# A hybrid block on one core: the second row tile scaled in two parts, a weight half rounded on another engine, rows turned together, and two Silus put off

## The chip, the cores and the metric

The program runs on one core of a Trainium2 chip. The metric is the device time of one execution in microseconds (us), the median of several runs. The core has five engines that each run their own queue in order: TensorE (PE; its weight loads are shown as PEld), VectorE (DVE), ScalarE (ACT), GpSimd (POOL) and SyncE (SP), which here only issues DMA transfers.

## What is computed

The reference is a decoder block on a residual stream x of 512 rows by 1024 columns. Cut to its stages:

```python
h = rmsnorm(x, norm1_g[l])
z = h @ w_in[l] + b_in[l]
z_glu, z_rx, z_rg, z_ga, z_gb = jnp.split(z, split_idx, axis=-1)
u = silu(layernorm(causal_depthwise_conv(glu(z_glu))))
y_a = u @ conv_w_out[l] + conv_b_out[l]
xb = causal_depthwise_conv(z_rx, lru_conv_w[l], lru_conv_b[l])
hb = rg_lru(xb, lru_wa[l], lru_ba[l], lru_wx[l], lru_bx[l], lru_lambda[l])
y_b = (hb * gelu(z_rg)) @ lru_w_out[l]
x = x + (sigmoid(z_ga) * y_a + sigmoid(z_gb) * y_b) @ w_mix_out[l]
h = rmsnorm(x, norm2_g[l])
x = x + (silu(h @ ffn_w1[l]) * (h @ ffn_w3[l])) @ ffn_w2[l]
return rmsnorm(x, norm_f_g)
```

Everything is float32. rg_lru has 16 heads of 80 columns, each with its own 80 by 80 gate weights and biases lru_ba and lru_bx; the channel mixer is 2816 wide.

## The kernel before

**Products.** Each float32 factor is split in a rounded high part and a low part (`split_to`, `first_parts`): a cast makes the high part, a subtraction the low part. A float32 product is then three products on TensorE: high by high, high by low, low by high (`mm3`). Names that end in h and l are these parts. Weights come in chunks of 128 by 1024 numbers: `load_chunk` loads a chunk to one of four `raw` buffers through SP's queue, `emit_chunk` makes its parts in one of five `hl` buffers, casts mostly on ScalarE, subtractions on POOL or DVE. `in0` is the first chunk of w_in; its parts are made in halves (`first_parts`, L131): first half cast on DVE (L133), subtracted on POOL (L119); then second half cast and subtracted on POOL.

**The start.** x lies in four row tiles of 128 rows (`xt`; the first three are in the `wsums` pool). Tiles 0 and 1 are normalised first: the sums of squares on DVE (`half_sum`) and ScalarE (`root`), the scaling by half tiles (`scale_half`, on DVE L672 or on ScalarE L670), then eight blocks of 128 by 128 per tile are turned by TensorE (`turn_rows`, L635) into PSUM banks. `spot` says where block c goes: with six banks, blocks 0 and 3 share bank 0, and 4 and 7 share bank 3. From there `turned_parts` makes h10h to h17h on ScalarE (L644) and h10l to h17l on DVE (L645), with the norm's weights from `par`. Thirteen products of ones (`warm`, L543) run on TensorE before that. `early_first` (L689) then takes the 24 products of the first chunk on the first 256 rows in an order that follows the arrival of their parts.

**Parameters.** The per-channel vectors are loaded as rows (`rowt`, `load_rows`) and turned by TensorE (`rows_turned`, L552) to columns of `par`: the 8 rows of norm1_g at the start, the other 400 later in four blocks, and a fifth block (L555) with lru_ba and lru_bx, which has a tile of its own (`heads_b`, named rowsh).

**Order.** Inside `tc.manual_schedule` the named engines keep the order of the code; elsewhere a scheduler orders by its own model and hands out buffer slots. `tc.issue_after(i)` queues what follows behind instruction i on its engine.

**The channel mixer** runs in steps k of 256 columns. Each step of class `Seven` takes seven products of half the size instead of eight (r1 to r7, 24 products on TensorE each), for which sums of weight quarters are made beforehand in pieces: `piece_load`, four sums (`piece_sums`), `piece_store` to DRAM. `out_step` walks these pieces for the last stage (`or`): the store of one, the sums of the next, the load of one more, the DMAs on POOL's queue. In a step, `first` combines r1 and r2 to c11, and `rest` makes q, c12 and c21; `out_of` applies the Silu on ScalarE (L1443) and multiplies on DVE (L1444). Weights for later products are cast on ScalarE meanwhile.

Of the kernel before, what the change touches and what calls it, by code (L numbers as in the profile page):

```python
# [13 lines left out]
P = 128  # L14
T = 512
# [13 lines left out]
NF = DF // P  # L29


SLOTS, SHORT = 63, 5
RAW = 4
HL = 5
AHEAD = 4
SUMS_BEHIND = 3
WARM = 13

PACK = HB // 2
ROWS_G = HB + PACK  # L40
# [4 lines left out]

PIECES = 3


OUT_PIECES = {0: "1", 1: "111", 2: "01", 3: "11", 4: "111", 5: "101", 6: "111", 7: "111", 8: "101", 9: "101", 10: "100"}
# [34 lines left out]
def tile_block(ctx, tc, a, out):  # L86
# [43 lines left out]

    def first_parts(h, l, full):  # L131
        for cs in (slice(0, T), slice(T, 2 * T)):
            (pool_e if cs.start else vec).tensor_copy(h[:, cs], full[:, cs])  # L133
            newest["sub"] = sub(pool_e, l[:, cs], full[:, cs], h[:, cs].bitcast(F32)).ins
        return h, l

# [361 lines left out]
        at += n  # L498
    rowt = [longt(f"rows{b}") for b in range(row_at(n_rows - 1)[0] + 1)]

    heads_b = longt("rowsh")

    pool_e.memset(heads_b[: 2 * NH, :P], 0.0)

    def load_head_rows():
        for g, name in enumerate(("lru_ba", "lru_bx")):
            nc.sync.dma_start(heads_b[g * NH : (g + 1) * NH, :HB], a[name][0].rearrange("(h p) -> h p", p=HB))

    def load_rows(i, queue=nc.sync):
        lo, m, src = parts[i]  # L510
# [1 line left out]
        queue.dma_start(rowt[b][r : r + m, :P], src)  # L512

    x_nat = a["x"].rearrange("b (t p) d -> p (b t) d", p=P)
    wide = [wsums.tile([P, 1024], F32, tag="wsum", name=f"x{t}") for t in range(PIECES)]
    xt = [[w[:, :T], w[:, T:]] for w in wide] + [[longt(f"x{t}{h}") for h in range(2)] for t in range(PIECES, NT)]

    def load_x(t):
        if t < PIECES:
# [19 lines left out]


    wp = bank2("warm")
    for _ in range(WARM):
        pe.matmul(wp[:, :P], ones, ones, start=True, stop=True)  # L543

    load_x(0)
    load_x(1)

    def rows_turned(c0, c1):
        pt = bank2(f"par_ps{c0}")
        for c in range(c0, c1, P):  # L550
            m = min(P, c1 - c)
            pe.transpose(pt[:, c - c0 : c - c0 + m], rowt[row_at(c)[0]][:m, :P], ident[:m, :m])  # L552
        at = T - 2 * NH
        if c0:
            pe.transpose(pt[:, at:], heads_b[: 2 * NH, :P], ident[: 2 * NH, : 2 * NH])  # L555
        (vec.tensor_copy if c0 else act.copy)(par[:, c0:c1], pt[:, : c1 - c0])
        if c0:
            act.activation(bh, pt[:HB, at:], AF.Copy, scale=0.5)

    def pc(name, i):  # L560
        return par[:, col[name] + i : col[name] + i + 1]
# [67 lines left out]
    def turn_rows(t, ps, half=None):  # L629

        some = (range(ND), (0, 3, 1, 2, 4, 7, 5, 6))[len(ps) == 6]
        for c in some if half is None else some[4 * half : 4 * half + 4]:
            b, at = spot(c, ps)
            at += P * (t % 2)
            pe.transpose(ps[b][:, at : at + P], xt[t][c // 4][:, (c % 4) * P : (c % 4 + 1) * P], ident)  # L635
# [71 lines left out]
    with tc.manual_schedule(engines={ET.PE, ET.Activation, ET.DVE, ET.SP, ET.Pool}):  # L707

        turned = [(bank if q < 5 else bank2)(f"tx0{q}") for q in range(6)]
        r0 = first_sums(0)  # L710
        vec.reciprocal(r0, r0)
        r1 = first_sums(1)
        scale_half(0, 0, r0)
        turn_rows(0, turned, 0)
        scale_half(0, 1, r0, True)
        rows_turned(0, n_first)
        vec.reciprocal(r1, r1)
        scale_half(1, 0, r1)
# [10 lines left out]
        early_first(lambda: (turn_rows(1, turned, 1), turned_parts(0, turned, range(4, ND))))  # L729
# [639 lines left out]

    def out_step(k):  # L1370
        due_sums(True)
        if out_at[1]:
            with tc.issue_after(newest["full"]):
                out_stores.append(piece_store(*out_at[1], pool_e).ins)
        if out_at[0]:
            sums_due.append([SUMS_BEHIND, out_at[0]])
        out_at[1], out_at[0] = out_at[0], None
# [39 lines left out]
    def f_product(k, got, ps, x_, w_, again=False, ahead=AHEAD, between=None):  # L1417
# [3 lines left out]
        for i in range(2):  # L1421
# [17 lines left out]
                emit_to(emitted[0] + 1)  # L1439
            due_sums()  # L1440

    def out_of(c, dst):
        act.activation(c[:, LO], c[:, LO], AF.Silu)  # L1443
        newest["now"] = vec.tensor_tensor(out=dst, in0=c[:, LO], in1=c[:, HI], op=ALU.mult).ins  # L1444

    class Seven:
# [36 lines left out]
        def rest(self):  # L1483
# [5 lines left out]
            act.copy(q, r1)  # L1489
            f_product(k, got, r5, "s1", "t1")  # L1490
            add(q, r5, q)
            c12 = shortt(f"c12_{k}")
# [58 lines left out]
    for k in range(KF):  # L1551
        if k in SEVEN:
            b = begun.pop(k, None)
            if not b:
                b = Seven(k)
                b.half()
                b.first()
                out_step(k)
            b.rest()
            continue  # L1560
# [145 lines left out]
```

## Time and profile before

| what | value |
|---|---|
| runs, us | 792.69, 788.48, 790.12; median 790.12 |
| profiled execution, us | 787.58 |
| its span, first to last instruction, us | 785.8 |
| mean granted TensorE clock | 0.999 |
| busy DVE, ACT, POOL, us | 679.3, 473.5, 362.9 |
| weight and sum DMA, mean | 253 GB/s |

The profile is of one execution. A row of the timeline or of the chain of waits gives start and duration in us, the engine, the line and the tile; in brackets behind a row of the timeline stands the idle time of the engine before it and what ended it. A matmul's duration is its latency, since products overlap: the distance from one start to the next is what it costs.

### The profile page before, as it was taken

The page shows a single profiled execution, that of the slowest core. Times are in us where ns is not written, and L with a number is a line of the kernel's source. Part 1 is how long each engine was busy: PE and PEld are TensorE (multiplying, and loading weights), DVE is VectorE, ACT ScalarE, POOL GpSimd, SP SyncE. Part 2 cuts the span into 40 slices and gives each one's busy share as a digit, 9 for nine tenths or more (in the row PEclk, how much of TensorE's full clock was granted, in tenths as well). Part 3 has the DMA queues.
Part 4 walks back from the last instruction along what each step waited for, and adds up shares of the span by engine and source line. Part 5 has one row for each costly group of instructions (what it writes and reads, how often), then busy time and mean ns, then how long its engine had stood idle before and what let it go on. Part 6 is the DMA issues. An engine that isn't in the chain of part 4 may idle for free.

```text
span 785.8 us, 12508 instructions
## 1 busy us (share of the span) xinstructions
PE 778.2 (99%) x4328; PEld 680.6 (87%) x4328; DVE 679.3 (86%) x1074; ACT 473.5 (60%) x696; POOL 362.9 (46%) x353
## 2 busy tenths in 40 slices
PE   9999999999999999999999999999999999999996
PEld 8988888888888888888888898999999999888885
DVE  6389998889987987999799869897887889999956
ACT  7543678966785786574245676445445555556844
POOL 4367876789788989754530380122323322000000
PEclk9999999999999999999999999999999999999999
DMA  7657989899999868998978575699999999878652
GB/s 225 189 144 211 267 225 269 230 277 272 260 266 280 266 195 251 309 299 285 314 252 297 172 216 181 193 306 307 308 335 331 314 315 318 268 235 278 194 172 108
DMA packets 188561, 199.04 MB, mean 253 GB/s; under 512 B 15290, under 2 KB 149586, under 8 KB 188498
## 3 DMA queue, kind: packets, MB, share of 16 engines
q1 hardware_dynamic: 178066, 161.80, 67.4%
q0 software_dynamic: 10272, 36.18, 13.9%
q8 instruction: 34, 0.56, 0.3%
q14 instruction: 29, 0.24, 0.1%
q10 hardware_dynamic: 160, 0.27, 0.1%
HBM read 146.30 MB, written 38.80 MB: 236 GB/s over the span
## 4 chain that ended last, share of the span: by engine, by line
PE 99%; DVE 0%; ACT 0%; issue 0%
PE z L573 36%; PE fr L1432 25%; PE or L1195 13%; PE yb L573 7%; PE ya L573 6%; PE mxr L1195 5%; PE f L573 3%; PE g L1021 2%; PE fr L1477 1%; PE warm L543 1%; PE tx L635 0%; PE th L618 0%; PE z L689 0%; ACT of L1647 0%; PE orl L1195 0%; PE par_ps L552 0%
## 5 line engine op out<-in xcount | busy, mean ns | idle before, releaser
L821 DVE SCALAR_TENSOR_TENSOR cv<-u,par,cv 128x507 f32<-128x507 f32 (+15 forms) x240 | 162.2, 733 | 4.2 <-ACT cv L817 3.3
L119 POOL TENSOR_TENSOR hl_in<-raw_in,hl_in 128x1024 fp32r<-128x1024 f32 (+1 forms) x52 | 123.3, 2382 | 54.5 <-ACT hl_in L123 40.7
L119 POOL TENSOR_TENSOR fws<-fws 128x256 f32<-128x256 f32 x114 | 92.4, 812 | 38.9 <-DMA fws<-in_ffn_w_dram 33.4
L413 POOL DMA_DIRECT2D ot<-fwso x21 | 15.4, 732 | 140.9 <-DVE fwso L119 140.9
L1432 PE MATMUL fr<-hs_0h,hl_ft 128*128 128x256 f32 x320 | 59.2, 283 | 0.0
L119 DVE TENSOR_TENSOR hl_ft<-raw_ft,hl_ft 128x1024 fp32r<-128x1024 f32 x39 | 47.6, 1219 | 6.1 <-ACT hl_ft L123 6.0
L123 ACT CAST hl_in<-raw_in 128x1024 fp32r<-128x1024 f32 x50 | 51.4, 1047 | 1.3 <-PE z L573 1.1
L1432 PEld LDWEIGHTS fr<-hs_0h,hl_ft 128*128 128x128 f32 x320 | 50.6, 192 | 0.0
L123 ACT CAST hl_ft<-raw_ft 128x1024 fp32r<-128x1024 f32 x40 | 41.2, 1044 | 10.8 <-PE fr L1432 7.9
L1432 PE MATMUL fr<-hs_0l,hl_ft 128*128 128x256 f32 x160 | 45.3, 283 | 0.0
L123 ACT CAST hl_fb<-raw_fb 128x1024 fp32r<-128x1024 f32 x30 | 31.4, 1048 | 20.1 <-DMA raw_fb<-in_ffn_w_dram 9.3
L573 PE MATMUL z<-h10h,hl_in 128*128 128x512 f32 (+1 forms) x108 | 41.1, 382 | 0.0
L573 PE MATMUL z<-h13h,hl_in 128*128 128x512 f32 (+1 forms) x108 | 40.8, 379 | 0.0
L573 PE MATMUL z<-h14h,hl_in 128*128 128x512 f32 (+1 forms) x108 | 40.8, 379 | 0.0
L573 PE MATMUL z<-h15h,hl_in 128*128 128x512 f32 (+1 forms) x108 | 40.8, 379 | 0.0
L573 PE MATMUL z<-h16h,hl_in 128*128 128x512 f32 (+1 forms) x108 | 40.8, 379 | 0.0
L573 PE MATMUL z<-h12h,hl_in 128*128 128x512 f32 (+1 forms) x108 | 40.8, 379 | 0.0
L573 PE MATMUL z<-h11h,hl_in 128*128 128x512 f32 (+1 forms) x108 | 40.8, 379 | 0.0
L573 PE MATMUL z<-h17h,hl_in 128*128 128x512 f32 (+1 forms) x108 | 40.8, 379 | 0.0
L119 POOL TENSOR_TENSOR hl_ot<-raw_ot,hl_ot 128x1024 fp32r<-128x1024 f32 x1 | 2.4, 2405 | 82.8 <-ACT hl_ot L123 82.8
L123 ACT CAST hl_ob<-raw_ob 128x1024 fp32r<-128x1024 f32 (+1 forms) x23 | 23.4, 1016 | 23.8 <-PE or L1195 12.6
L119 DVE TENSOR_TENSOR hl_fb<-raw_fb,hl_fb 128x1024 fp32r<-128x1024 f32 x29 | 35.3, 1221 | 2.4 <-ACT hl_fb L123 2.4
(948 smaller groups left out, 2635.7 us busy)
## 6 DMA issues: line engine op xcount, KB each, us to landing
raw_in<-in_w_in_dram SPq DMA_DIRECT2D x51, 512.0 KB
fws<-in_ffn_w_dram SPq DMA_DIRECT2D x38, 512.0 KB
raw_ft<-fs SPq DMA_DIRECT2D x34, 512.0 KB
fs<-fws POOLq DMA_DIRECT2D x25, 512.0 KB, 5.7
fwso<-in_ffn_w_dram POOLq DMA_DIRECT2D x42, 256.0 KB, 7.1
ot<-fwso POOLq DMA_DIRECT2D x21, 512.0 KB, 5.3
raw_ob<-in_ffn_w_dram SPq DMA_DIRECT2D x33, 256.0 KB
raw_ot<-ot SPq DMA_DIRECT2D x33, 256.0 KB
```

The source lines that it names most:

```text
L119: return eng.tensor_tensor(out=o, in0=x, in1=y, op=ALU.subtract)
L123: copy(h, full)
L413: return queue.dma_start(dest, raw.rearrange("p (m n) -> p m n", n=256))
L543: pe.matmul(wp[:, :P], ones, ones, start=True, stop=True)
L573: pe.matmul(ps, l, r, start=i == 0, stop=i == n - 1)
L821: vec.scalar_tensor_tensor(out=acc[:, s:], in0=u[c][:, : T - s], scalar=dw(c, s), in1=acc[:, s:], op0=ALU.mult, op1=ALU.add)
L1021: pe.matmul(ps[:HB], head_chunk[0][:ROWS_G, g, h % 2, m, :], ext[h][m][:ROWS_G], start=m == 0, stop=m == 1)
L1195: pe.matmul(banks[i][:, cs], l_[:, ts], r_[:, cs], start=start and n == 0, stop=stop and n == 2, skip_group_check=again)
L1432: pe.matmul(ps[:, HALVES[i]], lw[:, c, :], rx_, start=not (again or i or c or m), stop=bool(i and c == 3 and m == 2), skip_group_check=True,)
L1477: pe.matmul(self.r4[:, HALVES[i]], lw, rx_, start=not (i or c or m), stop=bool(i and c == 3 and m == 2), skip_group_check=True)
```

## The change

Its parts, in the order of the program:

- The warm products are cut in 8 and 5. Between them the 8 rows of norm1_g are turned, into the upper half of the sixth bank of `turned` instead of a bank of their own, and ScalarE copies them to `par` behind the first root instead of behind the scaling of tile 0.
- `turned` has seven banks; blocks 0 to 3 have one each, and 4 and 7 share one.
- The first half of tile 1 is scaled in two parts of 256 columns (`scale_part`), each followed by the turning of its two blocks; the second half of both tiles is turned behind that.
- The first half of in0's high part is cast by ScalarE instead of DVE.
- lru_ba and lru_bx are loaded to rows 32 to 63 of the last row tile, which has 16 rows of conv_dw_w, and turned with it in one block of 64 rows. Their own tile is gone.
- The pool of pieces has four buffers instead of three, the pool of long tiles 61 instead of 63.
- `out_step` issues the load of a piece ahead of the store, and loads run one piece further ahead.
- `left_over`: the Silu and multiplication of c11, and in most steps of c21, are put off until behind a later copy on ScalarE.

```diff
-SLOTS, SHORT = 63, 5
+SLOTS, SHORT = 61, 5
-WARM = 13
+WARM, WARM_LATER = 13, 5
-PIECES = 3
+PIECES = 4
     def first_parts(h, l, full):
         for cs in (slice(0, T), slice(T, 2 * T)):
-            (pool_e if cs.start else vec).tensor_copy(h[:, cs], full[:, cs])
+            (pool_e.tensor_copy if cs.start else act.copy)(h[:, cs], full[:, cs])
...
-    heads_b = longt("rowsh")
-
-    pool_e.memset(heads_b[: 2 * NH, :P], 0.0)
+    h_row = 2 * NH
+    pool_e.memset(rowt[-1][: 2 * h_row, :P], 0.0)
...
-            m = min(P, c1 - c)
+            m = 2 * h_row if c0 and c1 - c <= h_row else min(P, c1 - c)
             pe.transpose(pt[:, c - c0 : c - c0 + m], rowt[row_at(c)[0]][:m, :P], ident[:m, :m])
-        at = T - 2 * NH
-        if c0:
-            pe.transpose(pt[:, at:], heads_b[: 2 * NH, :P], ident[: 2 * NH, : 2 * NH])
+        at = c - c0 + h_row
...
-        return ((c % 4, c // 4 * 256), ((0, 1, 2, 0, 3, 4, 5, 3)[c], c in (3, 7) and 256))[len(ps) == 6]
+        return ((c % 4, c // 4 * 256), ((0, 1, 2, 3, 4, 5, 6, 4)[c], c == 7 and 256))[len(ps) == 7]
...
+    def scale_part(t, cs, r):
+        vec.tensor_scalar(out=xt[t][0][:, cs], in0=xt[t][0][:, cs], scalar1=r, scalar2=None, op0=ALU.mult)
...
         r0 = first_sums(0)
+        rows_turned(0, n_first, turned[5][:, 256:])
+        warm_products(WARM_LATER)
+        turned.append(bank2("tx06"))
         vec.reciprocal(r0, r0)
         r1 = first_sums(1)
         scale_half(0, 0, r0)
-        turn_rows(0, turned, 0)
+        turn_rows(0, turned, 0, 4)
         scale_half(0, 1, r0, True)
-        rows_turned(0, n_first)
         vec.reciprocal(r1, r1)
-        scale_half(1, 0, r1)
-        turn_rows(1, turned, 0)
+        for q in range(2):
+            scale_part(1, slice(256 * q, 256 * q + 256), r1)
+            turn_rows(1, turned, 2 * q, 2)
+        scale_half(1, 1, r1)
         emit_to(1)
-        scale_half(1, 1, r1)
-        turn_rows(0, turned, 1)
+        turn_rows(0, turned, 4, 4)
...
     def out_step(k):
         due_sums(True)
-        if out_at[1]:
-            with tc.issue_after(newest["full"]):
-                out_stores.append(piece_store(*out_at[1], pool_e).ins)
...
-            with tc.issue_after(([newest["full"]] * 2 + out_stores)[out_n[0]]):
+            with tc.issue_after(([newest["full"]] * 3 + out_stores)[out_n[0]]):
                 out_at[0] = piece_load(name, halves, pool_e), dest
             out_n[0] += 1
+        if stored:
+            with tc.issue_after(newest["full"]):
+                out_stores.append(piece_store(*stored, pool_e).ins)
...
+    left = []
+
+    def left_over(behind):
+        while left:
+            with tc.issue_after(behind):
+                out_of(*left.pop(0))
...
             self.c11 = shortt(f"c11_{self.k}")
-            act.copy(self.c11, self.r1)
+            left_over(act.copy(self.c11, self.r1).ins)
...
-    def first(self):
+    def first(self, wait=False):
             add(self.c11, self.r2, self.c11)
-            out_of(self.c11, self.uv[0][:, LO])
+            if wait:
+                left.append((self.c11, self.uv[0][:, LO]))
+            else:
+                out_of(self.c11, self.uv[0][:, LO])
...
-            act.copy(q, r1)
+            left_over(act.copy(q, r1).ins)
...
-            out_of(c21, v_[:, LO])
+            if k + 1 in SEVEN and k + 1 not in BEGUN + BEGUN_LATER:
+                left.append((c21, v_[:, LO]))
+            else:
+                out_of(c21, v_[:, LO])
```

Three places show how instructions move. The first is ScalarE's queue at the start, from the squares of tile 1 (n1j10) to the first rounded row block (h10h); the numbers behind names are buffers. Before:

```order
L661 ACTIVATE n1j10_191,stats_158<-x1_123 128x512
L662 ACTIVATE stats_158<-stats_158 128x1
L670 ACTIVATE x0_122<-x0_122,stats_158 128x512
L556 COPY par_114<-par_ps0_200 128x8
L644 ACTIVATE h10h_159<-tx00_177,par_114 128x256
```

Now:

```order
L560 COPY par_114<-tx05_176 128x8
L664 ACTIVATE n1j10_193,stats_152<-x1_122 128x512
L665 ACTIVATE stats_152<-stats_152 128x1
L676 ACTIVATE x0_121<-x0_121,stats_152 128x512
L133 CAST hl_in0_213<-raw_in0_210 128x512
L647 ACTIVATE h10h_153<-tx00_171,par_114 128x256
```

The copy of the parameters stands ahead of tile 1's squares, and the cast of the first weights' half has come between the scaling of tile 0 and h10h. Before, that cast stood in DVE's queue between the two scalings of tile 1.

The second place is SP's queue where the parameters' rows are loaded (rows1 to rows4) and the next weight chunks (raw_in16 is the fifth). Before, the end of these loads:

```order
L512 DMA rows1_116<-in_norm2_g_dram 8x128
L512 DMA rows1_116<-in_lru_conv_w_dram 16x128
L512 DMA rows2_117<-in_lru_conv_w_dram 24x128
L512 DMA rows2_117<-in_conv_dw_w_dram 104x128
L512 DMA rows3_118<-in_conv_dw_w_dram 128x128
L512 DMA rows4_119<-in_conv_dw_w_dram 16x128
L168 DMA raw_in16_526<-in_w_in_dram 128x8x128
```

Now, their beginning:

```order
L168 DMA raw_in9_229<-in_w_in_dram 128x8x128
L508 DMA rows4_119<-in_lru_ba_dram 16x80
L508 DMA rows4_119<-in_lru_bx_dram 16x80
L168 DMA raw_in16_525<-in_w_in_dram 128x8x128
L513 DMA rows1_116<-in_b_in_dram 52x128
L513 DMA rows1_116<-in_conv_dw_b_dram 8x128
```

The weight chunk raw_in16 has moved past the thirteen transfers of b_in to conv_dw_w.

The third place is ScalarE's queue in the channel mixer, where step 6 follows step 5 (fr are the products' banks, ft and fb weight chunks). Before:

```order
L1443 ACTIVATE c21_5_6040<-c21_5_6040 128x256
L1463 COPY c11_6_6118<-fr1_6_6087 128x512
L123 CAST hl_ft10_6_6122<-raw_ft10_6_6120 128x1024
L1443 ACTIVATE c11_6_6118<-c11_6_6118 128x256
L123 CAST hl_ft11_6_6172<-raw_ft11_6_6170 128x1024
L123 CAST hl_fb11_7_6190<-raw_fb11_7_6187 128x1024
L1489 COPY q_6_6221<-fr1_6_6087 128x512
```

Now:

```order
L1478 COPY c11_6_6115<-fr1_6_6084 128x512
L1458 ACTIVATE c21_5_6039<-c21_5_6039 128x256
L123 CAST hl_ft10_6_6121<-raw_ft10_6_6119 128x1024
L123 CAST hl_ft11_6_6169<-raw_ft11_6_6167 128x1024
L123 CAST hl_fb11_7_6187<-raw_fb11_7_6184 128x1024
L1507 COPY q_6_6218<-fr1_6_6084 128x512
L1458 ACTIVATE c11_6_6115<-c11_6_6115 128x256
```

The Silu of c21 (step 5) goes behind the copy of c11, and that of c11 from between two casts to behind the copy of q.

More of the change, by code (lines that the diff above doesn't have):

```diff
@@ L514, in tile_block @@
     x_nat = a["x"].rearrange("b (t p) d -> p (b t) d", p=P)
-    wide = [wsums.tile([P, 1024], F32, tag="wsum", name=f"x{t}") for t in range(PIECES)]
-    xt = [[w[:, :T], w[:, T:]] for w in wide] + [[longt(f"x{t}{h}") for h in range(2)] for t in range(PIECES, NT)]
+    WIDE = 3
+    wide = [wsums.tile([P, 1024], F32, tag="wsum", name=f"x{t}") for t in range(WIDE)]
+    xt = [[w[:, :T], w[:, T:]] for w in wide] + [[longt(f"x{t}{h}") for h in range(2)] for t in range(WIDE, NT)]
     def load_x(t):
-        if t < PIECES:
+        if t < WIDE:
             nc.sync.dma_start(wide[t], x_nat[:, t, :])
@@ L541, in tile_block, with warm_products, rows_turned @@
     wp = bank2("warm")
-    for _ in range(WARM):
-        pe.matmul(wp[:, :P], ones, ones, start=True, stop=True)
+    def warm_products(n):
+        for _ in range(n):
+            pe.matmul(wp[:, :P], ones, ones, start=True, stop=True)
+    warm_products(WARM - WARM_LATER)
     load_x(0)
     load_x(1)
-    def rows_turned(c0, c1):
-        pt = bank2(f"par_ps{c0}")
+    def rows_turned(c0, c1, pt=None):
+        if pt is None:
+            pt = bank2(f"par_ps{c0}")
         for c in range(c0, c1, P):
-            m = min(P, c1 - c)
+            m = 2 * h_row if c0 and c1 - c <= h_row else min(P, c1 - c)
             pe.transpose(pt[:, c - c0 : c - c0 + m], rowt[row_at(c)[0]][:m, :P], ident[:m, :m])
-        at = T - 2 * NH
-        if c0:
-            pe.transpose(pt[:, at:], heads_b[: 2 * NH, :P], ident[: 2 * NH, : 2 * NH])
+        at = c - c0 + h_row
         (vec.tensor_copy if c0 else act.copy)(par[:, c0:c1], pt[:, : c1 - c0])
         if c0:
-            act.activation(bh, pt[:HB, at:], AF.Copy, scale=0.5)
+            act.activation(bh, pt[:HB, at : at + h_row], AF.Copy, scale=0.5)
     def pc(name, i):
@@ L625, in spot, with turn_rows @@
     def spot(c, ps):
-        return ((c % 4, c // 4 * 256), ((0, 1, 2, 0, 3, 4, 5, 3)[c], c in (3, 7) and 256))[len(ps) == 6]
-    def turn_rows(t, ps, half=None):
-        some = (range(ND), (0, 3, 1, 2, 4, 7, 5, 6))[len(ps) == 6]
-        for c in some if half is None else some[4 * half : 4 * half + 4]:
+        return ((c % 4, c // 4 * 256), ((0, 1, 2, 3, 4, 5, 6, 4)[c], c == 7 and 256))[len(ps) == 7]
+    def turn_rows(t, ps, at=0, n=None):
+        for c in range(ND) if n is None else (0, 1, 2, 3, 4, 7, 5, 6)[at : at + n]:
             b, at = spot(c, ps)
@@ L728, in tile_block @@
         turned_parts(0, turned, range(4))
-        early_first(lambda: (turn_rows(1, turned, 1), turned_parts(0, turned, range(4, ND))))
+        early_first(lambda: (turn_rows(1, turned, 4, 4), turned_parts(0, turned, range(4, ND))))
         r2 = half_sum(2)
@@ L1371, in out_step @@
         due_sums(True)
-        if out_at[1]:
-            with tc.issue_after(newest["full"]):
-                out_stores.append(piece_store(*out_at[1], pool_e).ins)
-        if out_at[0]:
-            sums_due.append([SUMS_BEHIND, out_at[0]])
-        out_at[1], out_at[0] = out_at[0], None
+        stored, begun_ = out_at[1], out_at[0]
+        if begun_:
+            sums_due.append([SUMS_BEHIND, begun_])
+        out_at[1], out_at[0] = begun_, None
         steps = out_steps.get(k)
@@ L1556, in tile_block @@
                 b.half()
-                b.first()
+                b.first(True)
                 out_step(k)
```

3 lines of the change are left out of this document (2 added, 1 removed).

## The prediction

> **What bounds the kernel now.** I read the page's first part, then the chain of waits, then the timeline of the first 13 us, where most of the edit lies, and of one step of the channel mixer, where the rest lies.
>
> ```profile
> span 785.8 us, 12508 instructions
> PE 778.2 (99%) x4328; PEld 680.6 (87%) x4328; DVE 679.3 (86%) x1074; ACT 473.5 (60%) x696; POOL 362.9 (46%) x353
> ```
> ```profile
> 1.09 5.48 PE warm L543 x26
> 6.57 0.42 issue
> ...
> 7.62 0.15 PE par_ps L552
> ...
> 9.58 2.96 PE z L689 x23
> ...
> 15.41 1.75 PE tx L635 x16
> ...
> 22.91 0.49 PE par_ps L552 x4
> 23.40 0.08 PE par_ps L555
> ...
> 499.17 175.68 PE fr L1432 x1464
> ```
> TensorE is the bound: 778.2 of 785.8 us, and what it isn't busy is 1.09 us before the first instruction, 0.42 us at 6.57 and the tail. Busy could hide stalls, so I divide: 1464 products of 256 columns in 175.68 us are 0.120 us each over the whole channel mixer. Products this even leave nothing that other engines could give back. So an edit can win only where TensorE still waits, before 12.5 us, or by taking products away. It can lose anywhere.
>
> **The start.** The next rows decide the first chunk: who releases the first real product, and who the last ones.
>
> ```profile
> 6.78 0.71 ACT L670 ACTIVATE x<-x,stats 128x512 f32<-128x512 f32 x1
> 7.11 0.48 DVE L672 TENSOR_SCALAR x<-x,stats 128x512 f32<-128x512 f32 x1
> 7.51 0.42 DVE L133 CAST hl_in<-raw_in 128x512 fp32r<-128x512 f32 x1
> 8.01 1.45 POOL L119 TENSOR_TENSOR hl_in<-raw_in,hl_in 128x512 fp32r<-128x512 f32 x1 [6.58 <-DVE hl_in L133]
> 8.24 0.47 ACT L644 ACTIVATE h10h<-tx,par 128x256 fp32r<-128x256 f32 x1 [0.26 <-PE tx L635]
> 10.10 1.29 POOL L119 TENSOR_TENSOR hl_in<-raw_in,hl_in 128x512 fp32r<-128x512 f32 x1
> 11.20 0.61 ACT L138 CAST hl_in<-raw_in 128x512 fp32r<-128x512 f32 x1
> 11.44 0.19 PEld L689 LDWEIGHTS z<-h14h,hl_in 128*128 128x128 f32 x1
> ```
> Today the row tile x1 is scaled from 7.11 to 7.59, is turned, and ScalarE, which had stood 0.26 us for it, rounds h10h from 8.24 to 8.71; the first product follows at once. Scaled in parts of 256 columns, the first part should take between half of 0.48 us and the whole, say 0.33, so turning starts some 0.15 us sooner; with four banks for the first four blocks, h10h also waits for one block of its bank instead of two. The parameters' turning (0.15 us) has left this place. The two together, and ScalarE free of the parameters' copy, let h10h start at about 7.95 and the first product at about 8.5, some 0.3 us sooner; TensorE's turnings (1.75/16 = 0.11 us each) keep up with that.
>
> But it is a race of two chains. The weights' two low parts are POOL's, with a cast between them, from 8.01 to 11.39, and at 11.44 TensorE loads the first weights that need the last of them. They begin 0.08 us behind the rounding of the first half, which DVE ends at 7.93. On ScalarE that rounding stands behind the scaling that ends at 7.49; a cast of this shape took 0.61 us there (11.20), which gives 8.10; with DVE's 0.42 us it would be 7.91. POOL starts between 0.02 us sooner and 0.17 us later, and ends as much later. I take **+0.10 us** for the start, nearer to the row of the same engine: the 0.3 us won in front are lost waiting for POOL. Bounds: -0.3 if POOL gets through faster by as much (its first subtraction took 1.45 us and its second, of the same shape, 1.29), +0.3 if ScalarE's cast is drawn out.
>
> The warm products are cut in 8 and 5 with the 8-row turning between: 0.15 us at full speed, perhaps 0.3 there. The 0.42 us of idle at 6.57 covers it; without that cover it would cost just that. ScalarE's copy of the parameters moves into the 0.3 us in which ScalarE awaits x1.
>
> **The last rows.** The five blocks at 22.91 and 23.40 become four, the last of 64 columns instead of 16: 0.08 to 0.15 us less on TensorE's own path. I take **-0.10 us**.
>
> ```profile
> 14.36 0.29 SPq L512 DMA_DIRECT2D rows<-in_conv_b_out_dram  x1
> 15.94 0.28 SPq L512 DMA_DIRECT2D rows<-in_lru_conv_b_dram  x1
> ...
> 16.64 0.29 SPq L512 DMA_DIRECT2D rows<-in_norm_g_dram  x1
> ```
> ```profile
> DMA packets 188561, 199.04 MB, mean 253 GB/s; under 512 B 15290, under 2 KB 149586, under 8 KB 188498
> ```
> Two stretches of the same time, with the busy us of PE, PEld, DVE, ACT and POOL, the granted clock, the DMA engines' share and GB/s; and TensorE's sequencer at its waits for the rows:
>
> ```profile
> 14.50:15.90 1.40, 1.40 (x14) 1.40 (x13) 1.36 (x4) 1.25 (x3) 0.04 (x1) 1.00 0.32 78
> 15.90:18.40 2.50, 2.50 (x24) 2.50 (x23) 1.05 (x4) 2.45 (x6) 2.50 (x2) 1.00 0.05 12
> ```
> ```profile
> L552 PEldq EVENT_SEMAPHORE  x5: 51/51/51, 20.7 to 21.1; - x5
> ```
> With these rows goes a move that the diff doesn't show: on SP one weight chunk (512 KB) now goes ahead of thirteen row transfers instead of behind them. In the listing each transfer waits for the one eight places earlier (SP stands from 14.65 to 15.94 for that), so norm2_g (shown as norm_g) comes to wait for this chunk. The DMA engines are nearly empty from 14.5 to 18.4 (shares 0.32 and 0.05), so the chunk fills a hole: at the mean of 253 GB/s, 2.1 us behind 15.9, it lands by about 18.0. norm2_g then goes at 18.0 instead of 16.64, the rows land 1.35 us later, and TensorE's sequencer, which had seen the last of them at 21.1, sees it at 22.5, before the blocks' place at 22.9. Cost 0; without that cover, what is missing. Of POOL's and SP's other moves before 310 us, the nearest to TensorE puts four sums of a piece in front of a weight's low part:
>
> ```profile
> 186.02 2.39 POOL L119 TENSOR_TENSOR hl_in<-raw_in,hl_in 128x1024 fp32r<-128x1024 f32 x1
> ```
> ```profile
> 198.27 0.39 PE L573 MATMUL z<-h10h,hl_in 128*128 128x512 f32 x1
> ```
> A sum has 256 columns; at this row's rate (2.39 us for 1024) four are some 2.4 us. The low part that ends at 188.41 is first used at 198.27, so that is hidden four times over. Fewer long slots change who waits for whose slot, but add no instruction.
>
> **The channel mixer.**
>
> ```profile
> 583.95 0.42 ACT L1443 ACTIVATE c<-c 128x256 f32<-128x256 f32 x1 [2.37 <-DVE c L1144]
> 584.27 1.03 ACT L123 CAST hl_ft<-raw_ft 128x1024 fp32r<-128x1024 f32 x1
> ...
> 586.16 0.57 ACT L1489 COPY q<-fr 128x512 f32<-128x512 f32 x1
> ```
> ```profile
> 585.33 1.22 DVE L119 TENSOR_TENSOR hl_ft<-raw_ft,hl_ft 128x1024 fp32r<-128x1024 f32 x1 [0.51 <-ACT hl_ft L123]
> ```
> ```profile
> 588.29 0.28 PE L1432 MATMUL fr<-hs_1h,hl_ft 128*128 128x256 f32 x1
> ```
> ScalarE stands 2.37 us for a Silu whose input DVE makes, with the next weight cast queued behind it. Deferred behind the copy of q (586.16), that Silu no longer holds the cast. But the weights were in time already: DVE ends their low part at 586.55, and the second half of that block is used 12 products behind 588.29, at 589.73, with 3.2 us to spare. The number of instructions is the same; on POOL, loads pass stores in a queue that feeds pieces for the stage after 674 us. Gain 0, loss 0. What is queued behind the deferred product on DVE is the low part of the next step's second block. The Silu can be done by 586.73 + 0.42 = 587.15, and from 588.29 on TensorE still has three blocks of 24 products, 8.6 us, ahead of that weight, to 596.9: some 8 us cover it.
>
> **Sum.** 785.8 + 0.10 - 0.10 = 785.8 us of span. The profiled execution took 787.58 us, 1.78 us around its span; the median of the three runs is 790.12, 2.54 above that execution, and the runs scatter from 788.48 to 792.69. I carry that excess along: **790.1 us**.
>
> **Rivals.** *The clock opens later (8%).*
>
> ```profile
> L543 PE MATMUL warm<-ones x26: 275/421/582, 1.1 to 6.3; 128*128 128x128 f32 x26
> ```
> The warm products' records take 421 ns, the last of them 275: TensorE gets to full speed only near the end of the warm block, 5 us behind its start. If the turning inside the block set that back to about 10.8, the 16 blocks from 6.99 (6.57 + 0.42) on would go at half speed (0.22 us each), to 10.7 with the first product, and 23 products at 0.12 us would end at 13.5 instead of 12.54: about +1.0 us, 791.1. The block is as long as before, which speaks against it. The Trainium skill (TensorE: Matmul & The Clock Gate, Part 1 and Part 4) says that the gate looks at free-running windows of about 3.4 us and that transposes don't count as activity in the same way; by one such window it would be an estimated +0.4 us, and the trace agrees only that speed changes once, near 6 us.
>
> *The head start is kept (8%).* POOL's first subtraction takes 1.29 us like its second, or less: -0.3 - 0.10, 789.7.
>
> *The rows come late (3%).* The chunk lands after 18.4 and TensorE stands at 22.9: about +1, 791.1.
>
> *Runs come down to the profile (5%).* If the 2.5 us of excess are weights that are sometimes late, the longer margins in the mixer remove some: 788.5. The evenness of the profiled products doesn't show it.
>
> *The mixer turns slower (8%).* DVE's queue is in order, and seven steps (k = 4 to 10) now hold a product that waits for a Silu behind q's copy. If DVE thereby falls more than 3.2 us behind, TensorE stands at each step for the rest; 4 us late would be 7 x 0.8 = 5.6 us, 795.7. For it: DVE is busy 86% of the span. Against it: the Silu's input is old by then, and the weight behind it has 8 us.
>
> **Chances.** Forecast 68%, rivals as given. This kernel's measurement tells about 0.5%, 4 us, from no change. Only the mixer's rival passes that bound; with scatter I give slower 9%, faster 2% (the whole excess gone would be 0.3%), within 89%. The range takes the runs' own scatter, the start's bounds and the clock: 787.3 to 793.2.
>
> **What would show it.** Right: h10h starts near 7.95, the first product near 8.5, POOL's last low part ends near 11.5 and TensorE waits for it; four blocks at 22.8; products of 0.120 us from 499 on, and no Silu wait in front of the casts. Wrong: warm records of 421 ns followed by slow turnings, a gap at 22.7, any product rows above 0.12 us in the mixer, or POOL starting before 8.0.

## The result and the profile after

The changed kernel takes 787.60 us (median of 22 runs, 787.27 to 788.38); the kernel before, run beside it, 789.65 us (22 runs, 787.54 to 792.69). The ratio is 0.9975, with a 95% interval of 0.9967 to 0.9983: 2.05 us less. That is half of the 4 us within which the prediction speaks of no change, but with this many runs it is clear of noise. The lowest runs of both are the same within 0.3 us. What the change took away is the upper part of the scatter: 5.2 us before, 1.1 us now.

So the two profiled executions (787.58 us before, 787.45 now, spans 785.8 and 785.7) can't show it: the one before happened to be among its lowest runs. They do show the parts that the prediction worked out one by one. The chain of waits of the changed kernel (start, duration, work):

```profile
6.95 1.71 PE tx L638 x12
...
9.26 2.06 PE z L695 x16
11.36 1.10 PE z L695 x7
12.46 2.88 PE z L577 x24
...
22.84 0.53 PE par_ps L558 x4
23.37 49.50 PE z L577 x240
...
499.06 175.68 PE fr L1440 x1464
674.74 103.39 PE or L1204 x456
```

The second chunk starts at 12.46 us instead of 12.54, the run of 240 products behind the turned rows at 23.37 instead of 23.48, the channel mixer at 499.06 instead of 499.17 and lasts the same 175.68. All that the start and the rows gave in these two executions is 0.11 us, and nothing was added or lost behind it. The start's timeline, all engines:

```profile
7.41 0.60 ACT L133 CAST hl_in<-raw_in 128x512 fp32r<-128x512 f32 x1
7.92 0.47 ACT L647 ACTIVATE h10h<-tx,par 128x256 fp32r<-128x256 f32 x1
8.09 1.28 POOL L119 TENSOR_TENSOR hl_in<-raw_in,hl_in 128x512 fp32r<-128x512 f32 x1 [6.65 <-ACT hl_in L133]
8.44 0.39 PE L695 MATMUL z<-h10h,hl_in 128*128 128x256 f32 x1
...
10.01 1.30 POOL L119 TENSOR_TENSOR hl_in<-raw_in,hl_in 128x512 fp32r<-128x512 f32 x1
...
11.36 0.19 PEld L695 LDWEIGHTS z<-h14h,hl_in 128*128 128x128 f32 x1 [0.24 <-POOL hl_in L119]
```

The first product comes at 8.44 (before: 8.79), POOL's chain ends at 11.31 (before: 11.39), and TensorE stands 0.24 us for it at 11.36: the race of two chains went as told, with POOL the loser.

What differs between the two profiles, and is not in the chain, is what DVE waits for in the channel mixer. The view of DVE's waits from 520 to 680 us (who waits for what: us in total, times, longest), first before:

```profile
DVE fwso L119 <- DMA fwso<-in_ffn_w_dram: 10.8, 4, 3.6
DVE fws L119 <- DMA fws<-in_ffn_w_dram: 4.5, 1, 4.5
DVE hl_ft L119 <- ACT hl_ft L123: 3.8, 8, 0.5
```

and now:

```profile
DVE hl_ft L119 <- ACT hl_ft L123: 8.7, 16, 1.7
DVE hl_fb L119 <- ACT hl_fb L123: 7.9, 12, 1.2
```

Before, DVE stood 15.3 us for pieces on their way from DRAM (fwso for the last stage, fws for the mixer itself). Now it never does; it is early and waits for ScalarE's casts instead, which in turn wait for TensorE.

### The profile page after: what moved, and what is told of

It reads as the page before. It is cut to its first block, busy times and chain, and to the rows that moved or that the text cites. A ratio compares the mean times of both kernels' runs of the same rounds, so it can differ in the third digit from the quotient of the medians.

```text
span 785.7 us, 12502 instructions
## 1 busy us (share of the span) xinstructions
PE 777.9 (99%) x4327; PEld 680.0 (87%) x4327; DVE 682.8 (87%) x1074; ACT 474.6 (60%) x697; POOL 362.3 (46%) x353
## 4 chain that ended last, share of the span: by engine, by line
PE 98%; DMA 1%; DVE 0%; ACT 0%; SPq 0%; issue 0%
PE z L577 36%; PE fr L1440 25%; PE or L1204 13%; PE yb L577 7%; PE ya L577 6%; PE mxr L1204 5%; PE f L577 3%; PE g L1030 2%; PE fr L1495 1%; DMA x<-in_x_dram 1%; PE tx L638 0%; PE th L622 0%; PE z L695 0%; ACT of L1668 0%; PE orl L1204 0%; DVE n1j L659 0%
## 5 line engine op out<-in xcount | busy, mean ns | idle before, releaser
L119 DVE TENSOR_TENSOR hl_ft<-raw_ft,hl_ft 128x1024 fp32r<-128x1024 f32 x39 | 47.7, 1222 | 10.9 <-ACT hl_ft L123 10.8
L396 POOL DMA_DIRECT2D fwso<-in_ffn_w_dram x42 | 29.9, 716 | 23.7 <-DMA ot<-fwso 21.9
```

Of the source, the lines that this page charges most:

```text
L119: return eng.tensor_tensor(out=o, in0=x, in1=y, op=ALU.subtract)
L396: queue.dma_start(raw[:, h * n : h * n + n].rearrange("p (e n) -> p e n", n=256), src)
```

## The experiments

All kernels but the last two are the kernel before with one part of the change, or with one other thing moved. Each of the twelve has a profile and 11 or 12 runs; every ratio is to the kernel before, run on the same chip. Four chips were used, and the kernel before has medians of 789.22 to 790.00 us on them.

**Which part.** The kernel before once more, then three with one part each: the deferred products, the pieces, the start with the rows. Their diffs are those hunks of the diff above, of which these lines are the core:

```diff
# mixer_only
+    def left_over(behind):
+        while left:
+            with tc.issue_after(behind):
+                out_of(*left.pop(0))
# pieces_only
-SLOTS, SHORT = 63, 5
+SLOTS, SHORT = 61, 5
-PIECES = 3
+PIECES = 4
-            with tc.issue_after(([newest["full"]] * 2 + out_stores)[out_n[0]]):
+            with tc.issue_after(([newest["full"]] * 3 + out_stores)[out_n[0]]):
# start_only
-WARM = 13
+WARM, WARM_LATER = 13, 5
-            (pool_e if cs.start else vec).tensor_copy(h[:, cs], full[:, cs])
+            (pool_e.tensor_copy if cs.start else act.copy)(h[:, cs], full[:, cs])
+            scale_part(1, slice(256 * q, 256 * q + 256), r1)
-    heads_b = longt("rowsh")
```

> The kernel before, once more, to catch the work that differs between its own executions (its 22 runs scatter from 787.5 to 792.7 us, the changed kernel's from 787.3 to 788.4). All theories: ratio 1.000 within 0.002, runs scattering over 3 us or more. If the profile of this run falls above 789 us, theory A (weights of the channel mixer late now and then) expects fewer than 1464 products in 175.7 us there, the mixer's stretch from 499 on longer by most of the excess; theory B (the pieces for the stage after 674 us, waited for by DVE or POOL) expects the excess in or behind that stage; theory C (the start: when the clock opens, when x1 comes) expects it before 12.5 us, with all later work shifted by it; theory D (the rows late) expects TensorE standing at 22.9.

> The kernel before with the deferred products of the channel mixer alone (Silu behind the copy that follows). Theory A: nearly all of the 2.05 us comes from here, median 787.6 to 788.2, scatter about 1 us. Theories B, C, D: no difference from the kernel before, median near 789.6, scatter 4 to 5 us.

> The kernel before with the pieces alone: four piece buffers, each loaded one step sooner and ahead of the store, 61 long slots, and the first three row tiles in wide buffers as before. Theory B: median 787.6 to 788.2, scatter about 1 us. Theories A, C, D: median near 789.6, scatter 4 to 5 us.

> The kernel before with the start and the rows alone: warm products cut in two with the 8-row turning between, second row tile scaled in parts, first weight half rounded by ScalarE, heads' rows turned with the last rows. Theories C and D: median 787.6 to 788.2, scatter about 1 us. Theories A and B: within 0.2 us of the kernel before, scatter 4 to 5 us.

| kernel | median us | runs from, to | ratio, 95% interval |
|---|---|---|---|
| again | 788.72 | 787.30, 791.29 | 0.9978 to 1.0006 |
| mixer_only | 790.65 | 788.08, 792.81 | 1.0004 to 1.0030 |
| pieces_only | 787.70 | 787.45, 787.95 | 0.9961 to 0.9986 |
| start_only | 789.40 | 787.49, 792.00 | 0.9987 to 1.0013 |

The pieces alone are the whole result, in time and in scatter: theory B holds for the part, though not for the place, since the first stall below lies in the mixer, ahead of 674 us. The start and the rows alone gain nothing that these runs can tell. The deferred products alone gain nothing either: all four theories had them equal or faster, and they came out slightly slower, with 1 just outside the interval.

These profiles also caught what the first one had missed, since start_only's execution has a span of 788.0 us. Its timeline around 634 us, one fence for each engine. DVE:

```profile
628.94 1.22 DVE L119 TENSOR_TENSOR hl_fb<-raw_fb,hl_fb 128x1024 fp32r<-128x1024 f32 x1
634.10 0.89 DVE L119 TENSOR_TENSOR fwso<-fwso 128x256 f32<-128x256 f32 x2 [3.94 <-DMA fwso<-in_ffn_w_dram]
635.02 0.42 DVE L407 TENSOR_TENSOR fwso<-fwso 128x256 f32<-128x256 f32 x1
635.48 0.42 DVE L119 TENSOR_TENSOR fwso<-fwso 128x256 f32<-128x256 f32 x1
635.82 1.22 DVE L119 TENSOR_TENSOR hl_fb<-raw_fb,hl_fb 128x1024 fp32r<-128x1024 f32 x1
...
637.56 1.22 DVE L119 TENSOR_TENSOR hl_fb<-raw_fb,hl_fb 128x1024 fp32r<-128x1024 f32 x1
638.69 0.68 DVE L1152 TENSOR_TENSOR c<-fr,q 128x512 f32<-128x512 f32 x1
...
643.07 0.68 DVE L1152 TENSOR_TENSOR c<-fr,c 128x512 f32<-128x512 f32 x1
```

ScalarE:

```profile
629.09 1.05 ACT L123 CAST hl_fb<-raw_fb 128x1024 fp32r<-128x1024 f32 x1
633.38 1.05 ACT L123 CAST hl_fb<-raw_fb 128x1024 fp32r<-128x1024 f32 x1 [3.24 <-DMA raw_fb<-in_ffn_w_dram]
...
639.41 0.42 ACT L1451 ACTIVATE c<-c 128x256 f32<-128x256 f32 x1 [4.49 <-DVE c L1152]
...
643.79 0.42 ACT L1451 ACTIVATE c<-c 128x256 f32<-128x256 f32 x1 [1.27 <-DVE c L1152]
644.11 0.57 ACT L1471 COPY c<-fr 128x512 f32<-128x512 f32 x1
```

and TensorE:

```profile
642.97 0.28 PE L1440 MATMUL fr<-hs_1h,hl_fb 128*128 128x256 f32 x1
644.73 0.39 PE L1440 MATMUL fr<-hs_0h,hl_ft 128*128 128x256 f32 x1 [1.48 <-ACT c L1471]
```

Read from the top: DVE, in order, stands 3.94 us for a piece that is needed only after 674 us. Behind it in its queue stand the low part of weights that ScalarE had cast by 630.1 and the combinations of TensorE's results (c). ScalarE's Silus wait 4.49 and then 1.27 us for these combinations, so its copy out of a PSUM bank comes only at 644.11, and TensorE, which needs the bank, stands 1.48 us. ScalarE's own wait of 3.24 us for weights is not what ends last here: that cast is done at 634.43, and DVE takes up its low part only at 637.56. In the changed kernel the same two low parts start at 628.38 and 630.13, 7.4 us sooner:

```profile
628.38 1.23 DVE L119 TENSOR_TENSOR hl_fb<-raw_fb,hl_fb 128x1024 fp32r<-128x1024 f32 x1 [1.04 <-ACT hl_fb L123]
...
630.13 1.22 DVE L119 TENSOR_TENSOR hl_fb<-raw_fb,hl_fb 128x1024 fp32r<-128x1024 f32 x1
```

TensorE stands neither for the piece nor for the weights in the end: the order of two queues hands the delay on.

The profile of again shows another end of it: no stall in the mixer, but TensorE standing 0.50 us for DVE (x2b) at 722.46, and one or two tenths at low parts that DVE ends at 682.8 and 699.4. Each such wait also puts the next product back by some 0.1 us, and in all the last stage is 1.59 us longer than in the first profile. The view by stretches of the first profile tells why lateness out of the mixer can come up here (stretch, its length, DVE's busy time, clock, DMA share, GB/s):

```profile
680.00:720.00 40.00, 39.75 (x72) 1.00 0.79 253
```

DVE is busy nearly all of it, so it has no idle time in which to catch up.

How near the other executions were shows in a table that I worked out from the rows of each profile: from the end of DVE's low part of the second half of the first ft block of step k to the first product that uses it, in us.

| kernel | k=4 | 5 | 6 | 7 | 8 | 9 |
|---|---|---|---|---|---|---|
| before (787.58 us) | 5.4 | 3.2 | 2.8 | 5.4 | 4.0 | 2.7 |
| again (788.88 us) | 5.9 | 3.6 | 2.2 | 3.7 | 2.3 | 1.3 |
| start_only | 5.7 | 2.3 | 1.1 | 2.6 | 1.1 | 1.1 |
| changed kernel | 6.9 | 6.1 | 6.4 | 6.4 | 6.4 | 6.4 |

In the first three rows DVE stands for pieces, and the margin falls by 2 us or more from k = 4 to k = 5 and ends at 1 to 3 us; how far it falls differs from execution to execution. The changed kernel keeps its 6 us.

**Which edit of that part.** Three edits are in it: a fourth buffer, paid with two long slots, and the order of load and store on POOL.

```diff
# fourth_buffer and buffer_same_place
-SLOTS, SHORT = 63, 5
+SLOTS, SHORT = 61, 5
-PIECES = 3
+PIECES = 4
# fourth_buffer and load_first
-            with tc.issue_after(([newest["full"]] * 2 + out_stores)[out_n[0]]):
+            with tc.issue_after(([newest["full"]] * 3 + out_stores)[out_n[0]]):
# load_first, behind the load
-        if out_at[1]:
+        if stored:
             with tc.issue_after(newest["full"]):
-                out_stores.append(piece_store(*out_at[1], pool_e).ins)
+                out_stores.append(piece_store(*stored, pool_e).ins)
```

> The kernel before with the fourth piece buffer alone (61 long slots for it): a load may go before the transfer of one more store has landed, but on POOL it still stands behind the store of the piece two places ahead, which waits for DVE's sums. Theory O (the place in POOL's queue is the cause): nothing gained, median 789.0 to 789.8, scatter 4 us, DVE still standing some 11 us for loads of pieces. Theory P (the number of buffers is the cause): 787.6 to 788.0, scatter below 1 us, DVE's wait below 1 us.

> The kernel before with the order alone: three buffers as before, each load ahead of the store that it stood behind. Now a load waits on POOL until the store just ahead of it has landed (some 6 us), and goes then. Theory O: DVE's wait for loads shrinks from 11 us to below 3 us, median 787.6 to 788.2, scatter below 1.5 us. Theory P: POOL's waits for stores rise by 6 us a piece, the loads come no sooner, median 789 or more, scatter 4 us.

> The kernel before with the fourth piece buffer and 61 long slots, and POOL's queue exactly as before: store of piece n-2, then load of piece n. (In fourth_buffer the longer list of starting points had let the loads move ahead of that store as well.) Loop theory: load n waits for the sums of n-2, and at four pieces DVE waits for load n, so that a slow transfer is handed on from piece to piece; a buffer alone doesn't cut this, so DVE still stands 10 us or more for loads, median 789.0 to 790.0, scatter 3 us or more. Buffer theory (it is the fourth buffer or the fewer slots that count): 787.6 to 788.0, scatter below 1 us.

fourth_buffer took 787.66 us (787.23 to 788.04; ratio 0.9966 to 0.9984): the whole gain. But its profile shows that its description was wrong: load n goes directly behind the store of piece n-3, ahead of that of n-2 (at 39.0 us from the mixer's `f` products for the fourth piece, 0.7 us behind the first store), since the longer list of starting points lets the scheduler move it. So it wasn't the buffer alone, and buffer_same_place was made for that: 790.14 us (788.18 to 793.16; 1.0000 to 1.0027), no gain, which is what its loop theory told (789.0 to 790.0). load_first took 789.30 (787.70 to 792.03; 0.9988 to 1.0015), no gain either. POOL's loads (`fwso`) in the view by line (busy time, mean ns of one, then idle time before them and what ended it), load_first:

```profile
L396 POOL DMA_DIRECT2D fwso<-in_ffn_w_dram x42 | 30.0, 719 | 89.9 <-DMA ot<-fwso 74.7 <-DMA fs<-fws 14.6 <-issue 0.5
```

buffer_same_place, with its stores (`ot`):

```profile
L413 POOL DMA_DIRECT2D ot<-fwso x21 | 15.4, 734 | 153.0 <-DVE fwso L119 153.0
L396 POOL DMA_DIRECT2D fwso<-in_ffn_w_dram x42 | 29.8, 716 | 0.5 <-issue 0.5
```

Without the buffer, a load that is moved ahead waits on POOL until its buffer's store has landed, 74.7 us in all, and the stores behind it wait as well. Without the move, the buffer is free and the load stands behind a store that waits for DVE. It takes both; neither theory O nor theory P alone was right.

**By what way.** The loads' round is closed: sums of piece n on DVE, its store, the load of n+2 behind it, the sums of n+2. Three kernels move the sums, or that load, in the kernel before.

```diff
# sums_sooner
-SUMS_BEHIND = 3
+SUMS_BEHIND = 1
# sums_later
-SUMS_BEHIND = 3
+SUMS_BEHIND = 5
# later_with_filler, the fillers ahead of each load
-SUMS_BEHIND = 3
+SUMS_BEHIND, FILL = 5, 6
+            for _ in range(FILL):
+                with tc.issue_after(behind):
+                    behind = pool_e.memset(ones, 1.0).ins
```

> The kernel before with each piece's sums put two half blocks (some 2.9 us of TensorE's products) sooner into DVE's queue, nothing else changed. If DVE standing for a load of a piece, with weights' low parts queued behind, is the cause, this makes it worse: DVE's wait for loads rises from 11 us to 30 us or more, and the median to 791 or more. If the excess comes from anything else (the bandwidth, the weights' own transfers), it stays within 0.5 us of 789.5.

> The kernel before with each piece's sums two half blocks later in DVE's queue; POOL's queue is unchanged. Loop theory: sums, store and next load all move some 2.9 us later against TensorE, the low parts behind the sums lose 1.5 us or more of a margin that was 2.5 us in the first profile and near 0 in the second one; median 790.5 to 793. Waiting theory (only the time that DVE stands for loads counts): the loads have 2.9 us more before their sums, DVE stands less, median 787.6 to 788.5.

> As sums_later, and six memsets of a 128x128 tile that nobody reads any more are put on POOL between each piece's store and the load behind it, so that each load goes some 1.2 to 1.8 us later; every other engine's queue is as in sums_later. Read from the profiles so far, the round from a piece's sums over its store and the next load but one to that load's sums took 21.1 to 21.9 us where TensorE stalls (the kernel before, mixer_only, start_only, buffer_same_place) against 20.1 in sums_later and 20.8 in sums_sooner, and a step of TensorE takes 20.16 us. Loop theory: with 1.2 to 1.8 us more the round is above 21 us again, margins are eaten step by step, median 789 to 791 with a scatter of 2 us or more. Order theory (what counts is only behind which low parts the sums stand on DVE): 787.6 to 788.2, as sums_later.

All three came out at the changed kernel's time: 787.72 (787.40 to 788.53; 0.9969 to 0.9986), 787.79 (787.35 to 788.25; 0.9964 to 0.9985) and 787.74 us (787.40 to 789.04; 0.9964 to 0.9989). The first was expected to be worse, the second too by the loop theory, and the third by it again. In the third the loads did leave later (2.3 us behind the store of the thirteenth piece instead of 0.7), and one run of twelve reached 789.04, but the median didn't move. So the loop theory's forecasts failed, and not every standing of DVE costs time. Whether a round longer than a step of TensorE would, is not settled: the fillers put each load 1.6 us later behind its store, but from the sums of one piece to those of the third behind it (pieces 11 to 14) that kernel takes 19.3 to 21.0 us, where the kernel before takes 21.5 to 21.6 and a step 20.16. sums_sooner doesn't speak against the standing, since it shortened it (10.8 to 6.5 us) where it was expected to lengthen it. What had been written for sums_later as the waiting theory fits: DVE stands less there, and less at a time. The view of DVE's waits from 520 to 680 us, sums_later:

```profile
DVE fwso L119 <- DMA fwso<-in_ffn_w_dram: 4.2, 4, 2.0
```

later_with_filler:

```profile
DVE fwso L119 <- DMA fwso<-in_ffn_w_dram: 6.1, 7, 2.1
```

mixer_only:

```profile
DVE fwso L119 <- DMA fwso<-in_ffn_w_dram: 11.4, 4, 4.0
```

Put side by side from the same view. The stalls are TensorE's in the same execution: by how much the time from the first product of the sevenfold steps (`fr`, near 449.5 us) to the last of `or` exceeds the changed kernel's 329.84 us.

| kernel | DVE's standing for fwso, us | longest | stalls, us | median us |
|---|---|---|---|---|
| buffer_same_place (with 3.4 for a store) | 11.7 | 4.1 | 3.25 | 790.14 |
| mixer_only | 11.4 | 4.0 | 3.10 | 790.65 |
| start_only | 11.3 | 3.9 | 2.51 | 789.40 |
| before | 10.8 | 3.6 | 0.01 | 789.65 |
| again | 10.3 | 3.6 | 1.59 | 788.72 |
| load_first | 9.8 | 4.7 | 1.11 | 789.30 |
| sums_sooner | 6.5 | 2.1 | 0 | 787.72 |
| later_with_filler | 6.1 | 2.1 | 0 | 787.74 |
| sums_later | 4.2 | 2.0 | 0 | 787.79 |
| pieces_only, fourth_buffer, changed kernel | 0 | 0 | 0 | 787.70, 787.66, 787.60 |

The stalls account for what the five longer executions took, with spans of 786.8 to 789.1 us; the spans of all the others lie between 785.7 and 786.4. Every kernel in which DVE stands 3.6 us or more at a time has runs of 791 us and above; every one that stays below 2.2 us has its median at 787.6 to 787.8. (The single wait for fws, 1.8 to 5.6 us in those that have it, doesn't separate them: later_with_filler has 4.2 and load_first none.) Worked out as in the table of margins, later_with_filler has 3.2, 2.7, 4.3, 6.0, 6.9 and 6.0 us for k = 4 to 9: the margin falls and comes back. So short standings are made good, and long ones often not: the first profile has them and no stall, and load_first keeps 5 us of margin up to k = 8 and loses its time in the last stage alone. That is a regularity over these profiles, one for each kernel, found afterwards. Why the sums' old place gives the long standings, and the places on both sides of it short ones, stays open.

**The rest of the change.** The changed kernel without the deferral, and with DVE rounding the first half again:

```diff
# no_deferral (and first, rest without left)
-            left_over(act.copy(self.c11, self.r1).ins)
+            act.copy(self.c11, self.r1)
-            left_over(act.copy(q, r1).ins)
+            act.copy(q, r1)
# dve_rounds_first
-            (pool_e.tensor_copy if cs.start else act.copy)(h[:, cs], full[:, cs])
+            (pool_e if cs.start else vec).tensor_copy(h[:, cs], full[:, cs])
```

> The changed kernel without the deferred products of the channel mixer (Silu and product again at their old places); start, rows and pieces as changed. If the pieces alone carry the gain: median 787.5 to 787.8, no difference that can be measured from the changed kernel. If the deferral is needed beside them: above 788.2 with scatter of 2 us or more.

> The changed kernel with the first weights' first half rounded by DVE again, behind the scaling of x1 in parts and halves. POOL's chain should then start near 8.8 instead of 8.09 us and end some 0.7 us later, and TensorE, which in the changed kernel already stood 0.2 us for that chain near 11.2, waits for it: +0.5 to +0.7 us, median 788.1 to 788.3. If TensorE wasn't waiting for that chain: within 0.2 us of the changed kernel's 787.6.

no_deferral: 787.65 us (787.27 to 788.41; 0.9969 to 0.9988), so beside the pieces the deferral does nothing that can be measured. dve_rounds_first: 788.06 us (787.84 to 788.24; 0.9972 to 0.9992), 0.46 above the changed kernel, just below what was expected. Its timeline shows the path:

```profile
8.37 0.42 DVE L133 CAST hl_in<-raw_in 128x512 fp32r<-128x512 f32 x1
...
8.87 1.29 POOL L119 TENSOR_TENSOR hl_in<-raw_in,hl_in 128x512 fp32r<-128x512 f32 x1 [7.42 <-DVE hl_in L133]
...
12.14 0.19 PEld L695 LDWEIGHTS z<-h14h,hl_in 128*128 128x128 f32 x1 [0.48 <-POOL hl_in L119]
```

POOL starts 0.78 us later than in the changed kernel, and so do the weights that wait for it; 0.32 us of that is x, which came later in this execution (TensorE's turnings start at 7.27 instead of 6.95). TensorE stands 0.48 instead of 0.24 us. The two medians weren't taken side by side, but the profiles give the same: from the first turning of x to the first product of the sevenfold steps it takes 443.00 us here and 442.54 in the changed kernel (442.53 and 442.54 in start_only and no_deferral). POOL's chain does set the end of the first chunk, and with the scaling in parts the cast's place on ScalarE is worth some 0.46 us.

## Why the prediction was right, and where it wasn't

The forecast was no change, 790.1 us with a range of 787.3 to 793.2, and 0.89 for within 0.5%. Both held; the middle was 2.5 us too high, for a reason to which it had given 5%.

- **The bound.** TensorE sets the time, and "an edit can win only where TensorE still waits, before 12.5 us, or by taking products away": the first half held, the second was the reading that failed. The even 0.120 us per product was true of the profiled execution and was taken for all. The median before was 2.54 us above that execution, and the prediction says "I carry that excess along". It was stalls of TensorE in the mixer and in the last stage, and the change took them away: 789.65 - 787.58 = 2.07 us of excess over all runs before, 787.60 - 787.45 = 0.15 now. That is the term that was mis-sized: carried as 2.54, measured at 0.15. (0.47 of the 2.54 was the chance of three runs, whose median was 790.12.)
- **The pieces.** "on POOL, loads pass stores in a queue that feeds pieces for the stage after 674 us" was costed at nothing, on the ground of when the pieces are used. What they stood in front of in DVE's queue wasn't asked. The first profile has the row that asks it, in its list of waits: DVE's sums of fwso, 10.8 us for the DMA of fwso.
- **Runs come down to the profile (5%, 788.5 us).** This rival is what happened: weights that are sometimes late, and longer margins. It looked for the margins in the deferred Silus, though, and those give nothing (mixer_only, no_deferral). The result lies only 0.3 us above the lower end of the range, which stood for the runs' own scatter, so the range held partly by luck.
- **The start.** h10h at 7.92 (told: 7.95), first product at 8.44 (8.5), though in part by luck: 7.95 was worked out from x1's turning, and h10h's row shows no idle time before it, so that it follows the cast on ScalarE, which the prediction set to end at 8.10. In dve_rounds_first, without that cast, h10h waits for the turning and starts at 8.21, with x 0.32 us later, so both ways end at almost the same time. Further: POOL's start at 8.09 (between 7.99 and 8.18), its end at 11.31 (11.5). The first subtraction took 1.28 us instead of 1.45, as the rival of the kept head start supposed, so the term came out at -0.08 instead of +0.10. That TensorE waits for POOL was right, and dve_rounds_first shows it is that chain.
- **The last rows.** Told -0.10; from the first block to the next product the chain has 0.53 us (22.84 to 23.37) instead of 0.57 (22.91 to 23.48), so -0.04. The chunk that passes the rows on SP left no gap.
- **The clock.** The turnings from 6.95 on take 1.71 us for 12, not the 0.22 us each of the late clock. The Trainium skill (TensorE: Matmul & The Clock Gate, Part 4) says that transposes don't count as activity in the same way; a delay from the one inside the warm block is not in this trace, whose warm records get shorter at 4.99 us instead of 5.73. One execution couldn't settle it, though: in the ten profiles with the uncut warm block that change comes anywhere from 4.03 us to behind the block, so a single trace says little about this rival.
- **The mixer turns slower (8%).** It didn't: 175.68 us for 1464 products again. mixer_only has the smallest margins of all (0.3 us at k = 6, and below zero at k = 9) and a median 1.2 us above that of the kernel before on its chip, so without the pieces the deferral may cost something of the kind; no run here settles it.

## What to carry over

When the median of the runs lies above the profiled execution by more than the runs of a steady kernel scatter, take that excess for a term with a cause, and look for it in waits that the profile has but that don't yet reach the bound engine: an engine that stands in order for work needed much later is the first candidate, all the more when it has no idle time left in the stage behind. Ask of each such wait what is queued behind it, not when its own result is used. For a transfer that a busy engine stands for, a spare buffer and an earlier place in the issuing queue go together, since each alone did nothing here; moving the work that stands by two half blocks did as much without a buffer.

## What was not expected of the hardware

- With TensorE 99% busy and the same granted clock (0.997 to 0.999 in the twelve runs of again), executions of one kernel spread over 4 to 5 us. Half a piece (256 KB) took 7.3 us on average from issue to landing between 540 and 672 us of the first profile and 8.9 us at most, with the DMA engines 0.92 to 0.99 busy between 540 and 660 us. That the spread begins in such transfers is argued from DVE's waits, not shown by itself.
- The same subtraction of 512 columns on POOL, the first of in0, took 1.44 to 1.45 us in all ten profiles with the old start and 1.28 to 1.29 in all four with the new one. In the first profile it starts at 8.01 beside a scaling of x on DVE (7.84 to 8.32); in the changed kernel that scaling ends at 8.13, 0.04 us behind its start, and in dve_rounds_first before it. That this makes the difference is read from these rows and wasn't tried.
- The warm products' records change from 421 to 275 ns at a time that differs between executions of the same block: at 4.03 us in pieces_only, 5.73 in the kernel before and again, and not before the block's end at 7.0 in load_first and sums_sooner.
